# A trunk layer on one core: first two output tiles row by row, the last sums of x2 on VectorE, two PSUM banks for column tiles

## The chip, the core and the metric

The kernel runs on one core of a Trainium2 chip. The metric is the time of one execution in microseconds (us), measured on the device. A core has a matrix engine (TensorE, PE in the profile, with its weight loads as PEld), three elementwise engines (VectorE = DVE, ScalarE = ACT, GpSimd = POOL) and DMA queues, which SyncE (SP) feeds here. Matrix products land in PSUM, which has eight banks of 128 x 512 float32 values; everything else lies in SBUF.

## What is computed

One layer of a decoder trunk, for 512 positions of 2048 channels in float32:

```python
h = _rms_norm(x, norm1_g[l])
proj = h @ w_in[l]
aq, ak, av, bu, bg, cq, ck, cv = jnp.split(proj, splits, axis=-1)
...                                # A dilated attention, B GLU + conv + LayerNorm + swish, C sliding-window attention
mix = jnp.concatenate([out_a, out_b, out_c], axis=-1)
x = x + mix @ w_out[l]
h2 = _rms_norm(x, norm2_g[l])
x = x + (jax.nn.silu(h2 @ w_gate[l]) * (h2 @ w_up[l])) @ w_down[l]
```

The float32 precision is reached by splitting: every weight and operand becomes a high part (a rounded copy) and a low part (what the rounding left), and a product is a sum of several matmuls of parts.

## The kernel before

Everything lies transposed: channels on the 128 partitions, the 512 positions along the free axis. A *column tile* is 128 output channels by 512 positions and fills one PSUM bank. `mm3` (L254) adds one 128-row block of the contraction to it with three matmuls: high weight by high operand (L255), high weight by low operand (L256), low weight by high operand (L257).

Work goes in *units* of weights of 128 x 1024. A unit's weights arrive by a DMA that `pump` issues on SyncE's queue (L219); `split_up_to` makes the high part `wh` on ScalarE (L232, L237) and the low part `wl` by a subtraction on VectorE (L233, L238). From the third output tile of the second half on, that subtraction reads a second copy of the high part, `wn`, which lies in PSUM (L235, pool "high" with two buffers). `next_unit` hands a unit out and splits two units ahead.

1. **Projections** (61 units): one column tile after the other, each over 16 row blocks (`project`). Between them, as *ticks*, the mixers run. A tick is a point in the order of the program (`ticks.after(n, f)` emits f at the n-th tick from now), so a helper's place on each engine is fixed when the program is built. When a convolution pair `bu`, `bg` is there, `glu` multiplies both by the scale of the norm and with each other. The mixers' rows are the 16 row blocks c0 to a3, used in the order of `ROWS`; `split_mix` makes the high part `mh` (ScalarE) and the low part `ml` (VectorE, L746) of one.
2. **Output projection** (32 units, o tiles): half 0 uses the first eight rows for all 16 column tiles, then half 1 the other eight. `o0_n` is added to x in `residual` (L822), and `o1_n` to that (L825, tile `xr`), which gives x2. The last two mixer rows, a2 and a3, are still being computed in half 0; their matmuls, exponentials and transposes are emitted at the ticks of the first tile (one after each row) and of the others (one after each fourth row).
3. **x2's operands** during half 1: `scale_x2` makes h2 (scaled x2) and its square `sr` on ScalarE, one tick later `add_x2` makes differences of halves of h2 (`ta`, `tb`; L842 to L850), and `operands` their high and low parts (`h`, L814 on ScalarE and L815 on VectorE). These are operands of a Strassen-like scheme of seven products: `ssum2` sums the squares (L100). `add_x2` runs on GpSimd, for the very last tile (n = 15) on VectorE. `operand` q of pair j needs tiles j and j + 8, so the last pairs (6, 14) and (7, 15) come last.
4. **Gate, up and down**: for each of 44 gate and up groups and then 25 down groups, seven products in the order q = 5, 1, 7, 6, 2, 4, 3, one weight unit each, accumulate into banks `out0` to `out3` (`multiply`, L947). The weights of such a unit are sums of four blocks '11', '12', '21', '22' (GpSimd, L184; 's' is a running sum), queued in `sums` and emitted when the unit is due. For the first group, `norm2a` (after the third unit, q = 7) computes 1/rms of x2: `stat_rows` sums `ssum2` over partitions on PE (tile `n2s`, L295, in a buffer of pool "high"), VectorE scales (`n2v`, L361) and GpSimd takes the power (`n2r`, L362); `norm2b` (after the fourth unit, q = 6) spreads it over the partitions by four transposes on PE (L301).

PSUM: all eight banks are one pool (`bank`) at first, for column tiles and mixers alike, handed out in turn: a new tile waits until whatever held its bank was read. At the third o tile of half 1 the pool is closed; then four banks are `bank`'s and four hold the two buffers of "high".

Of the kernel before, what the change touches and what calls it, by code (L numbers as in the profile page):

```python
# [9 lines left out]
F32 = mybir.dt.float32  # L10
F32R = mybir.dt.float32r
# [4 lines left out]
P = 128  # L16
T = 512
# [28 lines left out]

N_SLOTS = 75

RAW_PLAIN = "22b sb 21 22a 11 sa 12".split()
# [70 lines left out]
def kernel(ctx: ExitStack, tc: tile.TileContext, xT, wi, wo, wgu, wd, cst_in, outT):  # L120
# [8 lines left out]
    def open_banks(**pools):  # L129
        if psum:  # L130
# [6 lines left out]
    open_banks(banks=8)  # L137
    ticks = Ticks()

    def slot(name, dt=F32, cols=T):  # L140
        return sp.tile([P, cols], dt, name=name, tag="s")

    def bank(name, cols=T):
        return psum["banks"].tile([P, cols], F32, name=name, tag="b")


# [5 lines left out]

    sums = defaultdict(list)
    raws, held = {}, {}

# [15 lines left out]
    def group(name, m, n, blocks):  # L171

        key = {k: (k, name) for k in ("11", "12", "21", "22", "s")}
        for k in ("21", "22", "11", "12"):
            entries.append((k + "ab"[m] if k == "22" else k, key[k], blocks[k]))
        u = len(works)

        def add(to, a, b, last=None):
            def go():
                if to == a:  # L180
                    out = raws[key[to]][0]
                else:
                    out = take("s" + "ab"[m], key[to], n)
                nc.gpsimd.tensor_add(out[:, :n], raws[key[a]][0][:, :n], raws[key[b]][0][:, :n])  # L184
                if last:
                    drop(key[last])
            return go

        sums[u - 4].append(add("s", "21", "22"))
        sums[u - 3].append(add("21", "21", "11"))  # L190
        sums[u].append(add("s", "s", "11", "11"))
        sums[u + 2].append(add("s", "s", "12"))
        works.extend((key[k], last, None) for k, last in (
            ("s", False), ("11", False), ("21", True), ("s", False), ("12", True), ("22", True), ("s", True)))
# [15 lines left out]

    splits = {}
    at = {"entry": 0, "split": 0, "use": 0}

    def pump(limit):
        while at["entry"] < len(entries) and len(raws) < limit and entries[at["entry"]][0] not in held:
            buf, key, parts = entries[at["entry"]]
            t, o = take(buf, key, sum(p.shape[-1] for p in parts)), 0
            for part in parts:
                nc.sync.dma_start(t[:, o:o + part.shape[-1]], part)  # L219
                o += part.shape[-1]  # L220
            at["entry"] += 1

    def split_up_to(i):
        while at["split"] <= min(i, len(works) - 1):
            key, last, eng = works[at["split"]]
            t, n = drop(key) if last else raws[key]
            u = at["split"]
            hi = wp.tile([P, 1024], F32R, name=f"wh{u}", tag="hi", bufs=SPLIT_BUFS)
            lo = wp.tile([P, 1024], F32R, name=f"wl{u}", tag="lo", bufs=SPLIT_BUFS)
            if eng or "high" not in psum:  # L230
                eng = eng or nc.vector
                nc.scalar.copy(hi[:, :n], t[:, :n])  # L232
                eng.tensor_sub(lo[:, :n], t[:, :n], hi[:, :n].bitcast(F32))  # L233
            else:
                near = psum["high"].tile([P, 1024], F32R, name=f"wn{u}", tag="h")  # L235
                nc.scalar.copy(near[:, :n], t[:, :n])
                nc.scalar.copy(hi[:, :n], t[:, :n])  # L237
                nc.vector.tensor_sub(lo[:, :n], t[:, :n], near[:, :n].bitcast(F32))  # L238
            splits[u] = (hi, lo)
            at["split"] += 1  # L240
# [4 lines left out]

    def next_unit():
        sums_now()
        u = at["use"]
        at["use"] += 1
        split_up_to(u + SPLIT_AHEAD)  # L250
        pump(RAW_EARLY if u < 20 else RAW_BUFS)
        return splits.pop(u)
# [111 lines left out]

    g4 = [bank(f"in{j}") for j in range(HEAD4)]
    h_hl = {}
# [30 lines left out]
    def project(name):  # L397
        b = bank(name)
        for half in range(2):
# [15 lines left out]

    def glu(j, bu, bg):
        t = slot(f"bg{j}")
        nc.vector.tensor_mul(t, bg, r1b)
        nc.scalar.activation(t, t, AF.Sigmoid)
        u = slot(f"bu{j}")  # L420
        nc.vector.tensor_mul(u, bu, r1b)
        nc.gpsimd.tensor_mul(u, u, t)
        hconv[j] = u

# [323 lines left out]

    ticks.after(1, spread_r1)
    ticks.after(2, glu, 0, g4[0], g4[1])  # L750
    ticks.after(2, glu, 1, g4[2], g4[3])
    g4 = None
# [12 lines left out]
    boxes = {"c": shared}  # L765
    part = {}
    for name in PROJ[HEAD4:]:
# [5 lines left out]
        if kind == "b":  # L773
            part[what + j] = b
            if what == "g":
                ticks.after(0, glu, int(j), part.pop("u" + j), part.pop("g" + j))
            continue
# [41 lines left out]
    def residual(n, b, half):  # L819
# [6 lines left out]
        nc.sync.dma_start(x2d[n], t)  # L826
        ticks.after(0, scale_x2, n)

    def scale_x2(n):
# [3 lines left out]
        nc.scalar.activation(sq if n else ssum2, t, AF.Square)  # L833
        ticks.after(1, add_x2, n, sq)

    def add_x2(n, sq):
        j = n % NJ
        eng = nc.gpsimd if n < KT - 1 else nc.vector
        if n < NJ:
# [4 lines left out]
        else:  # L844
# [15 lines left out]
    def split_rows(k):  # L860
        for name in ROWS[k:k + 3]:
            if name in mix:
                split_mix(name)

    load_x(0)
    load_x(1)
    late.append(True)
    for half in range(2):
        for i, n in enumerate(OUT_ORDER[half]):
            if half == 1 and i == 2:  # L870
# [30 lines left out]

    outs = [bank(f"out{i}") for i in range(4)]

# [227 lines left out]
    for g in range(2 * NP + len(DOWN)):  # L1131
# [8 lines left out]
        for i, q in enumerate(ORDER):  # L1140
# [113 lines left out]
```

## Time and profile before

| | |
|---|---|
| time, median of 3 runs (lowest, highest) | 1903.39 us (1902.68, 1906.31) |
| profiled execution: its own time, its span | 1905.27 us, 1903.5 us |
| PE busy, weight loads PEld | 1886.3 us (99%), 1638.7 us (86%) |
| DVE, ACT, POOL busy | 1443.3 us (76%), 1326.4 us (70%), 1179.6 us (62%) |
| granted PE clock, mean over the span | 0.998 of full speed |
| DMA moved | 317.67 MB, 167 GB/s |
| bytes read from HBM / written | 252.28 MB / 55.84 MB |

The first rows say how long the runs took; the profiled execution is one run more, and all durations in the text come from it. Its span covers the first to the last instruction, and the 1.8 us to its own time lie around it. The shares are averages: PE's 99% leaves about 17 us in which it had nothing to do, and the four engines are loaded differently from stage to stage. The projections end at about 411 us, the output projection at about 606 us, and the rest is the gate, up and down stage.

### The profile page before, as it was taken

How to read it: one execution, taken by the hardware profiler on the slowest of the kernel's cores; microseconds unless marked ns; L12 is line 12 of the kernel's file. 1: busy time of each engine (PE TensorE's matmuls, PEld its weight loads, DVE VectorE, ACT ScalarE, POOL GpSimd, SP SyncE). 2: the span in 40 equal slices, each digit the busy share in tenths (PEclk: the TensorE clock that was granted, in tenths of full speed). 3: DMA queues.
4: the chain of work that ended last, by engine and by line, in shares of the span. 5: the costliest groups of instructions: out<-in, count | busy, mean ns of one | idle time of the engine just before them, and what ended most of it. 6: DMA issues, size and time to landing. Idle time of an engine off the chain costs nothing.

```text
span 1903.5 us, 29681 instructions
## 1 busy us (share of the span) xinstructions
PE 1886.3 (99%) x10332; PEld 1638.7 (86%) x10332; DVE 1443.3 (76%) x2412; ACT 1326.4 (70%) x1850; POOL 1179.6 (62%) x801
## 2 busy tenths in 40 slices
PE   8999999999999999999999999999999999999999
PEld 7888888878887888888888888888888888888888
DVE  6788888997469777777777777777777866776777
ACT  6355654454356788888888888788887876767766
POOL 5134423331046787888787888788787655656777
PEclk9999999999999999999999999999999999999999
DMA  7343233323442335444454535444457766767777
GB/s 267 83 124 100 80 102 102 101 89 117 133 140 93 120 130 174 142 162 159 147 169 136 182 131 176 140 161 161 145 171 252 268 239 223 280 230 267 282 258 240
DMA packets 134246, 317.67 MB, mean 167 GB/s; under 512 B 15312, under 2 KB 30800, under 8 KB 134096
## 3 DMA queue, kind: packets, MB, share of 16 engines
q1 hardware_dynamic: 133952, 315.68, 49.5%
q8 instruction: 81, 1.33, 0.3%
q14 instruction: 69, 0.57, 0.1%
q10 hardware_dynamic: 144, 0.10, 0.0%
HBM read 252.28 MB, written 55.84 MB: 162 GB/s over the span
## 4 chain that ended last, share of the span: by engine, by line
PE 97%; DVE 2%; DMA 1%; issue 0%; SPq 0%; POOL 0%; ACT 0%; POOLq 0%; ACTq 0%; DVEq 0%
PE out L947 67%; PE o L256 3%; PE o L255 3%; PE o L257 3%; PE cq L255 2%; PE cq L257 2%; PE cq L256 2%; PE ak L255 1%; PE ak L257 1%; PE ak L256 1%; PE av L255 1%; PE av L256 1%; PE av L257 1%; PE aq L255 1%; PE aq L256 1%; PE aq L257 1%
## 5 line engine op out<-in xcount | busy, mean ns | idle before, releaser
L947 PE MATMUL out<-h,wh 128*128 128x512 f32 x2464 | 590.0, 391 | 0.9 <-DVE h L815 0.9
L947 PEld LDWEIGHTS out<-h,wh 128*128 128x128 f32 x2464 | 453.8, 189 | 89.1 <-DVE h L815 1.4
L947 PEld LDWEIGHTS out<-h,wl 128*128 128x128 f32 x2464 | 316.9, 192 | 12.0
L947 PE MATMUL out<-h,wl 128*128 128x256 f32 x2464 | 320.9, 283 | 0.0
L947 PE MATMUL out<-a,wh 128*128 128x512 f32 x1232 | 295.9, 391 | 0.0
L947 PEld LDWEIGHTS out<-a,wh 128*128 128x128 f32 x1232 | 225.8, 188 | 43.3
L232 ACT CAST wh<-w 128x1024 fp32r<-128x1024 f32 (+1 forms) x93 | 96.9, 1042 | 122.3 <-PE o L256 55.2
L947 PEld LDWEIGHTS out<-a,wl 128*128 128x128 f32 x1232 | 159.4, 191 | 6.9
L947 PE MATMUL out<-a,wl 128*128 128x256 f32 x1232 | 161.5, 283 | 0.0
L233 DVE TENSOR_TENSOR wl<-w,wh 128x1024 fp32r<-128x1024 f32 (+1 forms) x93 | 116.0, 1247 | 54.6 <-ACT wh L232 52.8
L432 DVE SCALAR_TENSOR_TENSOR y<-bu,cst,y 128x511 f32<-128x511 f32 (+14 forms) x120 | 89.9, 749 | 0.6
L960 DVE TENSOR_TENSOR y<-y,out 128x256 f32<-128x256 f32 x93 | 39.1, 420 | 43.4 <-PE out L947 37.9
L256 PE MATMUL o<-ml_c,wh 128*128 128x512 f32 x128 | 50.3, 393 | 3.1 <-DVE ml_c L746 3.1
L255 PE MATMUL cq<-hh,wh 128*128 128x512 f32 x128 | 51.2, 400 | 0.0
L255 PE MATMUL o<-mh_c,wh 128*128 128x512 f32 x128 | 51.0, 398 | 0.0
L257 PE MATMUL cq<-hh,wl 128*128 128x512 f32 x128 | 50.0, 391 | 0.0
L257 PE MATMUL o<-mh_c,wl 128*128 128x512 f32 x128 | 50.0, 391 | 0.0
L256 PE MATMUL cq<-hl,wh 128*128 128x512 f32 x128 | 49.9, 390 | 0.0
L961 DVE TENSOR_TENSOR y<-y,out 128x256 f32<-128x256 f32 x101 | 42.5, 421 | 3.5
L842 POOL TENSOR_TENSOR ta<-h 128x256 f32<-128x256 f32 x8 | 7.3, 910 | 58.5 <-issue 44.9
L354 POOL TENSOR_TENSOR ssum<-ssum,sq 128x512 f32<-128x512 f32 x15 | 25.1, 1676 | 22.4 <-ACT sq L353 22.0
L660 POOL TENSOR_SCALAR a3e<-a3e,a3d 128x128 f32<-128x128 f32 (+3 forms) x8 | 9.2, 1152 | 36.4 <-DVE a3d L658 26.8
(3125 smaller groups left out, 4998.9 us busy)
## 6 DMA issues: line engine op xcount, KB each, us to landing
a<-od SPq DMA_DIRECT2D x168, 256.0 KB, 5.4
od<-a SPq DMA_DIRECT2D x147, 256.0 KB, 4.7
w<-in_wi SPq DMA_DIRECT2D x59, 512.0 KB, 3.7
w<-in_wo SPq DMA_DIRECT2D x32, 512.0 KB, 3.6
yd<-y SPq DMA_DIRECT2D x68, 128.0 KB, 3.0
y<-yd SPq DMA_DIRECT2D x34, 256.0 KB, 5.3
x<-in_xT SPq DMA_DIRECT2D x16, 256.0 KB, 7.2
xr<-in_xT SPq DMA_DIRECT2D x16, 256.0 KB, 3.8
```

The source lines that it names most:

```text
L232: nc.scalar.copy(hi[:, :n], t[:, :n])
L233: eng.tensor_sub(lo[:, :n], t[:, :n], hi[:, :n].bitcast(F32))
L255: nc.tensor.matmul(out, wh, xh, start=start, stop=False)
L256: nc.tensor.matmul(out, wh, xl, start=False, stop=False)
L257: nc.tensor.matmul(out, wl, xh, start=False, stop=stop)
L354: eng.tensor_add(acc, acc, sq)
L432: nc.vector.scalar_tensor_tensor(yconv[j][:, i:], hconv[j][:, :T - i], c, yconv[j][:, i:], op0=ALU.mult, op1=ALU.add)
L660: nc.gpsimd.tensor_scalar(e[:, o:o + n], e[:, o:o + n], rd[:, i:i + 1], None, op0=ALU.mult)
L842: eng.tensor_sub(n1, h11, h12)
L947: nc.tensor.matmul(out, lhs[:, s], rhs, start=begin, stop=last and low == flip[0] and x is xs[-1], skip_group_check=True)
L960: sign(out, out if first is None else first, main)
L961: sign(out, out, rest)
```

## The change

1. *First two tiles row by row.* `first_two` holds o0_0 and o0_1 open together in two banks: for each of the eight rows it adds the row to both tiles, then ticks. Before, tile 0 took all eight rows with a tick after each, and tile 1 followed with two ticks.
2. *x2's last sums.* `add_x2` of pair (6, 14) moves from GpSimd to VectorE, as (7, 15) was. The `scale_x2` and `add_x2` of n = 15 come at once, without ticks between. The sums into `ssum2` of the squares of tiles 7, 14 and 15 are VectorE's. The last o tile ticks after every second row.
3. *First weight sum and copies.* The running sum 's' += '11' of the first gate group is emitted at the start of o1_15 (`first_sum`) instead of with its unit, and the `wn` copies of the next two units right after o1_15's matmuls (`near_of`).
4. *Banks.* Two banks, handed out in turn by `column`, belong to column tiles alone throughout (projections, o tiles, `out0` and `out1`, `in0`); the mixers' pool has six, and two from the third o tile of half 1 on (`out2`, `out3`).
5. `glu_u` multiplies `bu` as soon as it is there; `glu` then needs `bg` alone.
6. `norm2a` and `norm2b` run one unit later (after q = 6 and after q = 2).

```diff
+    psum["tiles"] = ctx.enter_context(tc.tile_pool(name="tiles", bufs=COLUMN_BANKS, space=bass.MemoryType.PSUM))
+    open_banks(banks=8 - COLUMN_BANKS)
...
+    def column(name):
+        return psum["tiles"].tile([P, T], F32, name=name, tag="c")
...
-        sums[u].append(add("s", "s", "11", "11"))
+        (sums[u] if name != f"g{GU_ORDER[0]}" else first_sum).append(add("s", "s", "11", "11"))
...
+    def near_of(u, t, n):
+        if u not in nears:
+            nears[u] = psum["high"].tile([P, 1024], F32R, name=f"wn{u}", tag="h")
+            nc.scalar.copy(nears[u][:, :n], t[:, :n])
...
-        ticks.after(0, scale_x2, n)
+        if n < KT - 1:
+            ticks.after(0, scale_x2, n)
+        else:
+            scale_x2(n)
...
-        eng = nc.gpsimd if n < KT - 1 else nc.vector
+        eng = nc.gpsimd if n < KT - 2 else nc.vector
...
-            ticks.after(1, operands, j, (7, n3), (6, n2), (2, h21))
+            soon = n < KT - 1
+            ticks.after(soon, operands, j, (7, n3), (6, n2), (2, h21))
             ticks.after(2, operands, j, (4, n4), (3, h22))
-        if n:
-            ticks.after(1, eng.tensor_add, ssum2, ssum2, sq)
+        if n == NJ - 1:
+            ticks.after(4, nc.vector.tensor_add, ssum2, ssum2, sq)
+        elif n:
+            ticks.after(1 if eng is nc.gpsimd else 2, eng.tensor_add, ssum2, ssum2, sq)
...
+    def first_two(*ns):
+        two = [((bank if i else column)(f"o0_{n}"), *next_unit(SPLIT_AHEAD - i)) for i, n in enumerate(ns)]
+        for k in range(8):
+            row = ROWS[k]
+            while row not in m_hi and row not in mix:
+                ticks.tick()
+            split_rows(k)
+            s = slice(k * P, (k + 1) * P)
+            for b, wh, wl in two:
+                mm3(b, wh[:, s], wl[:, s], m_hi[row], m_lo[row], k == 0, k == 7)
+            ticks.tick()
+        for i, n in enumerate(ns):
+            residual(n, two[i][0], 0)
+            load_x(i + 2)
...
-                open_banks(banks=4, high=2)
-            b = bank(f"o{half}_{n}")
+                open_banks(banks=4 - COLUMN_BANKS, high=2)
+            b = column(f"o{half}_{n}")
             wh, wl = next_unit()
+            if half == 1 and i == KT - 1:
+                first_sum.pop()()
...
-                if kk % 4 == 3 or i == 0:
+                if kk % 4 == 3 or i == 0 or (half == 1 and n == KT - 1 and kk % 2):
                     ticks.tick()
+            if half == 1 and i == KT - 1:
+                for u in range(at["split"], at["split"] + 2):
+                    near_of(u, *raws[works[u][0]])
...
-    outs = [bank(f"out{i}") for i in range(4)]
+    outs = [(column if i < COLUMN_BANKS else bank)(f"out{i}") for i in range(4)]
...
-            if g == 0 and i in (2, 3):
-                (norm2a, norm2b)[i - 2]()
+            if g == 0 and i in (3, 4):
+                (norm2a, norm2b)[i - 3]()
```

PE at the start of the output projection, before. The numbers behind names count buffers; `mh_c0` is row c0's high part, `wh61` and `wl61` are tile 0's weights, and `a2o`, `a2ph`, `a2pl` belong to the mixer row a2.

```order
L255 MATMUL o0_0_4235<-mh_c0_4146,wh61_4037 128x512
L256 MATMUL o0_0_4235<-ml_c0_4147,wh61_4037 128x512
L257 MATMUL o0_0_4235<-mh_c0_4146,wl61_4038 128x512
L700 MATMUL a2o0_4249<-a2ph00_4119,av20_3696 128x512
L701 MATMUL a2o0_4249<-a2pl00_4152,av20_3696 128x512
```

And after:

```order
L266 MATMUL o0_0_4238<-mh_c0_4149,wh61_4040 128x512
L267 MATMUL o0_0_4238<-ml_c0_4150,wh61_4040 128x512
L268 MATMUL o0_0_4238<-mh_c0_4149,wl61_4041 128x512
L266 MATMUL o0_1_4245<-mh_c0_4149,wh62_4126 128x512
L267 MATMUL o0_1_4245<-ml_c0_4150,wh62_4126 128x512
L268 MATMUL o0_1_4245<-mh_c0_4149,wl62_4127 128x512
L712 MATMUL a2o0_4256<-a2ph00_4122,av20_3699 128x512
```

Between two ticks of row a2 there now stand six matmuls of o tiles where three stood.

VectorE at the end of the output projection, before. `xr15` is x2's last tile, `o1_15` the last o tile; `wl95` is the low part of the third gate unit (q = 7), `h7_6` the operand q = 7 of pair 6.

```order
L815 TENSOR_TENSOR h5_7_5862<-ta7_5836,h5_7_5862 128x256
L825 TENSOR_TENSOR xr15_5026<-xr15_5026,o1_15_5840 128x512
L238 TENSOR_TENSOR wl95_5933<-w('21', 'g1')_5438,wn95_5934 128x1024
L815 TENSOR_TENSOR h7_6_5952<-ta6_5790,h7_6_5952 128x256
L815 TENSOR_TENSOR h6_6_5955<-tb6_5882,h6_6_5955 128x256
```

And after:

```order
L825 TENSOR_TENSOR h7_6_5883<-ta6_5793,h7_6_5883 128x256
L825 TENSOR_TENSOR h6_6_5886<-tb6_5873,h6_6_5886 128x256
L825 TENSOR_TENSOR h2_6_5889<-h2_14_5863,h2_6_5889 128x256
L101 TENSOR_TENSOR ssum2_4215<-ssum2_4215,sr7_5824 128x512
L825 TENSOR_TENSOR h4_6_5899<-tb6_5873,h4_6_5899 128x256
L825 TENSOR_TENSOR h3_6_5902<-h2_14_5863,h3_6_5902 128x256
L101 TENSOR_TENSOR ssum2_4215<-ssum2_4215,sr14_5864 128x512
L835 TENSOR_TENSOR xr15_5019<-xr15_5019,o1_15_5843 128x512
L864 TENSOR_TENSOR ta7_5839<-h2_7_5823,h2_15_5912 128x256
```

The add of the last x2 tile stood ahead of pair 6's operands and now stands behind them, behind pair 6's three differences and behind two sums into `ssum2`.

VectorE around the second norm, before. `wl97` and `wl98` are the low parts of the gate units q = 2 and q = 4, `g1u` and `g1r` sums of the group's products.

```order
L100 TENSOR_TENSOR ssum2_4212<-ssum2_4212,sr15_5963 128x512
L815 TENSOR_TENSOR h4_7_6016<-tb7_5980,h4_7_6016 128x256
L815 TENSOR_TENSOR h3_7_6019<-h2_15_5962,h3_7_6019 128x256
L955 TENSOR_REDUCE g1u_6023<-out1_5890 128x256
L238 TENSOR_TENSOR wl97_6026<-w('12', 'g1')_5642,wn97_6027 128x1024
L361 TENSOR_SCALAR n2v_6054<-n2s_6049 128x4
```

And after:

```order
L825 TENSOR_TENSOR h4_7_6010<-tb7_5916,h4_7_6010 128x256
L825 TENSOR_TENSOR h3_7_6013<-h2_15_5912,h3_7_6013 128x256
L101 TENSOR_TENSOR ssum2_4215<-ssum2_4215,sr15_5913 128x512
L998 TENSOR_REDUCE g1u_6026<-out1_5922 128x256
L249 TENSOR_TENSOR wl97_6029<-w('12', 'g1')_5645,wn97_6030 128x1024
L998 TENSOR_REDUCE g1r_6055<-out2_5923 128x256
L1003 TENSOR_TENSOR g1r_6055<-g1r_6055,out0_5921 128x256
L1004 TENSOR_TENSOR g1r_6055<-g1r_6055,out0_5921 128x256
L249 TENSOR_TENSOR wl98_6060<-w('22', 'g1')_5496,wn98_6061 128x1024
L372 TENSOR_SCALAR n2v_6086<-n2s_6081 128x4
```

The last sum of squares has moved behind h4 and h3, and `n2v`, which PE's sum of `ssum2` feeds, behind `wl98`.

More of the change, by code (lines that the diff above doesn't have):

```diff
@@ L47 @@
 N_SLOTS = 75
+COLUMN_BANKS = 2
 RAW_PLAIN = "22b sb 21 22a 11 sa 12".split()
@@ L129, in open_banks @@
     def open_banks(**pools):
-        if psum:
+        if "stack" in psum:
             psum.pop("stack").close()
@@ L135, in open_banks @@
                 tc.tile_pool(name=f"{name}{len(pools)}", bufs=bufs, space=bass.MemoryType.PSUM))
-    open_banks(banks=8)
+    psum["tiles"] = ctx.enter_context(tc.tile_pool(name="tiles", bufs=COLUMN_BANKS, space=bass.MemoryType.PSUM))
+    open_banks(banks=8 - COLUMN_BANKS)
     ticks = Ticks()
@@ L153 @@
     sums = defaultdict(list)
+    first_sum = []
     raws, held = {}, {}
@@ L209 @@
                                                   for i in range(2) for k in range(2)})
-    splits = {}
+    splits, nears = {}, {}
     at = {"entry": 0, "split": 0, "use": 0}
@@ L234, in split_up_to @@
             else:
-                near = psum["high"].tile([P, 1024], F32R, name=f"wn{u}", tag="h")
-                nc.scalar.copy(near[:, :n], t[:, :n])
+                near_of(u, t, n)
+                near = nears.pop(u)
                 nc.scalar.copy(hi[:, :n], t[:, :n])
@@ L244, in sums_now, with next_unit @@
             fn()
-    def next_unit():
+    def next_unit(ahead=SPLIT_AHEAD):
         sums_now()
@@ L249, in next_unit @@
         at["use"] += 1
-        split_up_to(u + SPLIT_AHEAD)
+        split_up_to(u + ahead)
         pump(RAW_EARLY if u < 20 else RAW_BUFS)
@@ L363, in token_scale @@
         return v, r
-    g4 = [bank(f"in{j}") for j in range(HEAD4)]
+    g4 = [(column if j < COLUMN_BANKS - 1 else bank)(f"in{j}") for j in range(HEAD4)]
     h_hl = {}
@@ L397, in project @@
     def project(name):
-        b = bank(name)
+        b = column(name)
         for half in range(2):
@@ L414, with glu_u, glu @@
     hconv, yconv = {}, {}
-    def glu(j, bu, bg):
+    def glu_u(j, bu):
+        u = hconv[j] = slot(f"bu{j}")
+        nc.vector.tensor_mul(u, bu, r1b)
+    def glu(j, bg):
         t = slot(f"bg{j}")
@@ L419, in glu @@
         nc.scalar.activation(t, t, AF.Sigmoid)
[L420 to L423, printed above, removed]
+        nc.gpsimd.tensor_mul(hconv[j], hconv[j], t)
     def tap(j, i):
@@ L749 @@
     ticks.after(1, spread_r1)
-    ticks.after(2, glu, 0, g4[0], g4[1])
-    ticks.after(2, glu, 1, g4[2], g4[3])
+    for j in range(2):
+        ticks.after(2, glu_u, j, g4[2 * j])
+        ticks.after(2, glu, j, g4[2 * j + 1])
     g4 = None
@@ L765 @@
     boxes = {"c": shared}
-    part = {}
     for name in PROJ[HEAD4:]:
@@ L773 @@
         if kind == "b":
-            part[what + j] = b
-            if what == "g":
-                ticks.after(0, glu, int(j), part.pop("u" + j), part.pop("g" + j))
+            ticks.after(0, glu if what == "g" else glu_u, int(j), b)
             continue
@@ L833, in scale_x2 @@
         nc.scalar.activation(sq if n else ssum2, t, AF.Square)
-        ticks.after(1, add_x2, n, sq)
+        if n < KT - 1:
+            ticks.after(1, add_x2, n, sq)
+        else:
+            add_x2(n, sq)
     def add_x2(n, sq):
         j = n % NJ
-        eng = nc.gpsimd if n < KT - 1 else nc.vector
+        eng = nc.gpsimd if n < KT - 2 else nc.vector
         if n < NJ:
@@ L869 @@
         for i, n in enumerate(OUT_ORDER[half]):
+            if half == 0 and i < 2:
+                if i == 0:
+                    first_two(*OUT_ORDER[0][:2])
+                continue
             if half == 1 and i == 2:
```

## The prediction

> **What bounds the kernel now.** I read the page first: the engines' shares and the chain of work that ended last.
>
> ```profile
> PE 1886.3 (99%) x10332; PEld 1638.7 (86%) x10332; DVE 1443.3 (76%) x2412; ACT 1326.4 (70%) x1850; POOL 1179.6 (62%) x801
> PE 97%; DVE 2%; DMA 1%; issue 0%; SPq 0%; POOL 0%; ACT 0%; POOLq 0%; ACTq 0%; DVEq 0%
> ```
>
> PE is busy for 1886.3 of 1903.5 us, and the change removes no matmul. So it can only act through PE's 17 us of idle time and through PE's clock. I asked next for PE's waits (engine, tile and line, what ended the wait, total us, count, mean):
>
> ```profile
> PE in L255 <- ACT wh L232: 5.3, 1, 5.3
> PE o L256 <- DVE ml_c L746: 3.1, 3, 2.5
> PE n2s L295 <- DVE ssum L100: 2.0, 1, 2.0
> PE out L947 <- DVE h L815: 0.9, 1, 0.9
> PE o L255 <- DVE xr L825: 0.9, 1, 0.9
> ```
>
> The first is the start of the program, which stays. The other four, 6.9 us, lie where the change works: the first o tile, the third tile of half 1, and the passage from the output projection to the gate stage. Then the clock, by windows of 3.41 us (window, its length, busy time of PE, PEld, DVE, ACT, POOL, then the granted clock):
>
> ```profile
> 415.68:419.10 3.42, 1.86 (x9) 1.37 (x10) 3.42 (x6) 1.14 (x3) 2.56 (x1) 1.00 0.47 95
> 545.81:551.25 5.44, 5.44 (x25) 4.51 (x24) 5.07 (x7) 3.72 (x9) 3.07 (x3) 1.00 0.41 145
> 613.66:617.07 3.41, 1.45 (x9) 1.21 (x9) 3.41 (x4) 1.54 (x2) 2.44 (x1) 1.00 0.00 0
> 617.07:623.90 6.83, 6.52 (x23) 5.90 (x24) 5.30 (x10) 1.99 (x2) 3.94 (x3) 0.50 0.26 79
> ```
>
> The clock fell to half once, for 6.83 us, behind a stretch of 3.41 us in which PE was busy for 1.45. A stretch with 1.86 busy cost nothing. So 1.96 us of idle time in 3.41 tripped it here and 1.56 did not. The fall cost half of the 6.52 busy us, 3.3. The second row is one undisturbed o tile: 24 matmuls in 5.44, 0.227 each.
>
> **First two tiles (part 1).** PE at rows c0 to c6 of tile 0 (start, duration, line, operation; in brackets the idle time before and its releaser), then VectorE:
>
> ```profile
> 411.44 0.39 PE L255 MATMUL o<-mh_c,wh 128*128 128x512 f32 x1
> 412.12 0.39 PE L700 MATMUL a2o<-a2ph,av 128*128 128x512 f32 x1
> 413.38 0.40 PE L255 MATMUL o<-mh_c,wh 128*128 128x512 f32 x1
> 416.95 0.50 PE L256 MATMUL o<-ml_c,wh 128*128 128x512 f32 x1 [2.47 <-DVE ml_c L746]
> 418.30 0.33 PE L676 MATMUL a2t<-ident,a2e 128*128 128x128 f32 x1 [0.29 <-POOL a2e L660]
> 422.23 0.50 PE L256 MATMUL o<-ml_c,wh 128*128 128x512 f32 x1 [0.21 <-DVE ml_c L746]
> 424.06 0.50 PE L256 MATMUL o<-ml_c,wh 128*128 128x512 f32 x1 [0.41 <-DVE ml_c L746]
> 416.21 1.70 DVE L746 TENSOR_TENSOR ml_c<-mix_c,mh_c 128x512 fp32r<-128x512 f32 x2
> ```
>
> Idle: 2.47+0.29+0.21+0.41 = 3.38. Row c2's low part is made on VectorE whatever PE does, and is there just before 416.95. After the change PE has six matmuls for c0, the mixer's products (412.12 to 413.38, 1.26), six for c1 and one for c2 before it needs that part: 411.44 + 13 x 0.227 + 1.26 = 415.65. It waits 1.2 to 1.3 instead of 2.47. Each later row has three more matmuls (0.68) ahead of it, more than any of the three small waits, so they go. That is 2.1 of idle time; with the slower restarts behind three gaps (the duration is 0.50 there, 0.39 elsewhere, 0.1 each) and bunched transposes I take 2.6, from 2.1 to 3.0. The a2 and a3 work comes a tile later; o tiles without a wait cover it, and without that cover the 1.2 would come back.
>
> **Banks at the third tile of half 1 (part 4).**
>
> ```profile
> 529.37 0.47 PE L255 MATMUL o<-mh_a,wh 128*128 128x512 f32 x1 [0.87 <-DVE xr L825]
> ```
>
> Here the pool of eight is closed, and the tile in the new pool waits for the add that reads the tile before. The column banks now persist, and the other bank of the two was read a tile earlier: 0.9 gained. It is lost again if the ring of two binds elsewhere (a rival below). `glu_u` (part 5) I cost at nothing: the projections show no PE wait in the list but the first, and the multiply only moves forward.
>
> **The passage into the gate stage (parts 2, 3, 4, 6).** VectorE, GpSimd and PE before:
>
> ```profile
> 600.60 1.51 DVE L815 TENSOR_TENSOR h<-ta,h 128x256 fp32r<-128x256 f32 x1
> 602.03 0.67 DVE L825 TENSOR_TENSOR xr<-xr,o 128x512 f32<-128x512 f32 x1
> 602.63 1.21 DVE L238 TENSOR_TENSOR wl<-w('11', 'g1')_5541,wn 128x1024 fp32r<-128x1024 f32 x1
> 610.74 0.41 DVE L815 TENSOR_TENSOR h<-h,h 128x256 fp32r<-128x256 f32 x1
> 611.07 0.41 DVE L848 TENSOR_TENSOR ta<-h,h 128x256 f32<-128x256 f32 x1
> 611.52 0.43 DVE L849 TENSOR_TENSOR tb<-ta,h 128x256 f32<-128x256 f32 x1
> 616.65 0.68 DVE L100 TENSOR_TENSOR ssum<-ssum,sr 128x512 f32<-128x512 f32 x1
> 600.35 1.48 POOL L100 TENSOR_TENSOR ssum<-ssum,sr 128x512 f32<-128x512 f32 x1
> 613.67 2.44 POOL L184 TENSOR_TENSOR w('s', 'g1')_5693<-w('s', 'g1')_5693,w('12', 'g1')_5642 128x1024 f32<-128x1024 f32 x1 [3.81 <-ACT h L814]
> 613.79 2.60 DVE L815 TENSOR_TENSOR h<-tb,h 128x256 fp32r<-128x256 f32 x1
> 607.51 2.00 PE L947 MATMUL out<-h,wh 128*128 128x512 f32 x8
> 610.30 2.68 PE L947 MATMUL out<-h,wh 128*128 128x512 f32 x11
> 617.38 1.87 PE L295 MATMUL n2s<-ones,ssum 128*128 128x1 f32 x8 [2.00 <-DVE ssum L100]
> 624.52 2.08 PE L947 MATMUL out<-h,wh 128*128 128x512 f32 x8
> ```
>
> An `h` subtraction takes 0.41, but 2.60 beside GpSimd's sum (613.79 beside 613.67): it ends when that ends. I carry this over. *First*, GpSimd now has the 2.4-us weight sum at 600.4, in place of the 1.48 of `ssum`; VectorE's subtraction of 600.60 ends at 603.1 instead of 602.1. Behind it stand, by the distances between starts, xr14 0.60, wl94 1.13, two h 0.68, three differences 1.25, three h 1.02, a sum 0.60, two h 0.68, a sum 0.60: 6.56. So xr15 is added from 609.7 to 610.3; before, this stood ahead of pair 6.
>
> That makes a **new wait**. The second column bank, `out1`, is o1_15's bank, so q = 1's first matmul waits for xr15's add. The eight matmuls at 607.51 are the last four of q = 5 and the first four of q = 1, so q = 1 started at 608.42; likewise q = 7 at 611.21, 2.79 a unit. Now it stalls from 608.4 to 610.3, 1.9 us; if the weight sum blocks nothing, 0.9. Three units then end at 610.3 + 8.37 = 618.7, and their operands are ready sooner (ta7 at 611.07 as before).
>
> *Second*, VectorE from 611.07: differences 1.25, wl95 1.13, three h 1.02, wl96 1.13, one h 0.34, to 615.95. The next h stands beside GpSimd's sum of '12', which waits for wl96, and ends with it at about 618.4. Then `ssum2` 0.60, a reduction 0.60, wl97 1.2: 620.85. `n2s` now stands behind `wn98` in the pool "high", so it takes the buffer of `wn97`, and PE's sum of squares waits for **wl97**, not for `ssum2` alone: 618.7 to 620.9, 2.2 us idle. What is queued behind it on PE is the whole unit q = 2. That unit ends at about 624.4; `n2v`, behind wl98, and the power give `n2r` at 624.65, the spread ends at 625.1. Before, spread and q = 2 ended at 624.52 + 2.79 = 627.3. So the stage gains 2.2 at a full clock, the cold 3.3 of before being gone; with a fall as before (idle 2.2 against the 1.96 that tripped it) it loses 0.9, the wait for `n2r` being absorbed.
>
> The Trainium skill, "TensorE: Matmul & The Clock Gate", section "Why this matters for your kernels", advises against PE-idle gaps over about 3 us, since one idle window sends the clock back to half. By that rule a gap of 2.2 does not trip it, and the sum would be the second case below. This trace speaks against the rule as a threshold: the gap of 2.00 (with 0.94 before it) tripped the clock.
>
> **Sum.** The profiled execution took 1905.27 (span 1903.5 and 1.8 around it), 1.9 above the median of 1903.39; its waits are taken as those of the median too. 2.6 + 0.9 - 0.9 = 2.6: **1900.8 us**.
>
> **The rivals.**
>
> *The clock stays up.* If the gap of 2.2 is split over two windows, or the limit is higher, the stage gains 2.2: 2.6 + 0.9 + 2.2 = 5.7, 1897.7 us. For it: 1.56 idle in a window did nothing. Against it: 1.96 did.
>
> *GpSimd goes first.* The first weight sum of the up group needs a block whose DMA is issued when wl95 has let a buffer go (613.5).
>
> ```profile
> w('22', 'u1')_5940<-in_wgu SPq DMA_DIRECT2D x1, 512.0 KB, 4.4
> ```
>
> With 0.4 of issue and 4.4 of transfer it lands at 618.3 to 618.5, just when `ssum2` wants to start at 618.4. If the weight sum starts first, `ssum2` ends with it at about 621.4 and wl97 at 623.2: idle 4.5, no gain at full clock (-0.1), and the clock surely falls (-3.1). 3.5 - 3.2 = 0.3: 1903.1 us. The Trainium skill, "SBUF — State Buffer", section "Who interferes with whom", says that issue order decides which of a two-input VectorE operation and a reading GpSimd operation blocks fully; the 2.60 above agrees. The stall of q = 1 tripping the clock as well (1.9 idle) would cost about the same.
>
> *The ring of two binds (slower).* Each o tile now waits for the add of the tile two before. VectorE's add of an `xr` needs no more than its place:
>
> ```profile
> 598.14 0.67 DVE L825 TENSOR_TENSOR xr<-xr,o 128x512 f32<-128x512 f32 x1
> 600.21 0.39 PE L255 MATMUL o<-mh_a,wh 128*128 128x512 f32 x1
> ```
>
> That add ends at 598.81, 1.4 before PE starts o1_15, the user of its bank. Once adds end over 5.44 us, one tile, after their tile, PE stalls. With VectorE 1.5 late at four tiles, 6.0, and a cold 3.3, against 3.5: 5.8 over, about 1909. Against it: pair 6's work falls on VectorE only at the last tile.
>
> *The first part does nothing*: the rows behind c2 wait as much as before because the low parts come later with the order, and the passage comes out even: 1903.4.
>
> **How the numbers follow.** Forecast 0.38; clock stays up 0.25; GpSimd first 0.19; ring 0.10; nothing 0.08. A measurement of this kernel can tell about 0.2% (3.8 us) from no change: faster is below 1899.6. The forecast's terms vary by 2 us, so a third of it is faster (0.13), all but 0.01 of the second case (0.24), together 0.37, say 0.38. Slower: the ring 0.10, and of GpSimd first with both falls and of nothing 0.06: 0.16. The rest is 0.46. The range takes in the second case with part 1 at its upper bound, 1897.7 - 0.4 - 1 for the shorter stall = 1896.3, rounded down to 1896.0, and GpSimd first with a second fall, 1903.1 + 3.1 = 1906.2, rounded to 1906.0; it leaves out the ring and the tails.
>
> **What would show it.** Right: PE's wait for ml_c falls to one of about 1.3; none for `xr` at the third tile of half 1; a new wait of `out` for `xr` near 605, of 0.9 to 1.9 us; `n2s` waiting 2 us or more for a low part `wl`. The granted clock behind it tells the forecast from the second case, the start of `ssum2`'s last sum against GpSimd's tells the third. Wrong: waits of o tiles for `xr` in half 1, or PE waits among the projections.

## The result and the profile after

The changed kernel took 1899.22 us (median of 8 runs, 1897.87 to 1901.06) against 1903.53 us (8 runs, 1902.68 to 1906.31): ratio 0.9977, 95% interval 0.9966 to 0.9988, 4.3 us less. The profiled execution took 1898.99 us; its span is 1897.2. PE's shares and waits in it, from the page and the view of waits:

```profile
PE 1883.3 (99%) x10332; PEld 1637.2 (86%) x10332; DVE 1442.8 (76%) x2417; ACT 1325.7 (70%) x1850; POOL 1173.0 (62%) x796
PE in L266 <- ACT wh L243: 5.3, 1, 5.3
PE n2s L306 <- DVE wl L249: 2.0, 1, 2.0
PE out L990 <- DVE xr L835: 1.8, 1, 1.8
PE o L267 <- DVE ml_c L758: 1.1, 1, 1.1
```

The three waits for ml_c are one of 1.1; the wait for `xr` at the third tile of half 1 is gone; two waits in the passage are new, and so is what they wait for. PE's starts of the same matmuls in the two traces show where the time went:

| point of the program | lead of the changed kernel, us |
|---|---|
| first o matmul (411.44 before, 409.90 after) | 1.54 |
| o tiles, 500 to 525 us | 4.54 |
| first gate matmul (605.65 before, 599.96 after) | 5.69 |
| rest of the gate stage, to the end | 6.28 |

So the first two tiles gave 3.0, the third tile of half 1 gave 1.15, the passage 0.6, and 1.54 stood ahead of them. Of that, 0.35 is how the program started, which differs from execution to execution (from -0.87 to 0.53 in the other traces below). The rest came at three places of the projections (208, 221 and 349 us), 0.85 of it at 349 us, where the kernel before has a wait that the changed kernel lacks:

```profile
349.48 0.33 PE L676 MATMUL a0t<-ident,a0e 128*128 128x128 f32 x1 [0.63 <-POOL a0e L660]
```

The traces show 6.3 where these medians show 4.3: the profiled execution of before was 1.7 above the median of the eight runs here. Three larger sets of runs of before, below, have medians of 1904.2 to 1904.9, so 4.3 is rather a low value. The passage after, PE's rows:

```profile
599.96 1.07 PE L990 MATMUL out<-h,wh 128*128 128x512 f32 x4
604.71 1.19 PE L990 MATMUL out<-h,wh 128*128 128x512 f32 x4 [1.80 <-DVE xr L835]
615.34 1.05 PE L306 MATMUL n2s<-ones,ssum 128*128 128x1 f32 x8 [1.98 <-DVE wl L249]
620.70 0.60 PE L312 MATMUL n2s<-ident,n2r 128*128 128x128 f32 x4
```

VectorE's and GpSimd's:

```profile
594.90 2.62 DVE L825 TENSOR_TENSOR h<-ta,h 128x256 fp32r<-128x256 f32 x1
603.98 0.68 DVE L835 TENSOR_TENSOR xr<-xr,o 128x512 f32<-128x512 f32 x1
610.32 2.63 DVE L825 TENSOR_TENSOR h<-h,h 128x256 fp32r<-128x256 f32 x1
612.88 0.68 DVE L101 TENSOR_TENSOR ssum<-ssum,sr 128x512 f32<-128x512 f32 x1
614.08 1.21 DVE L249 TENSOR_TENSOR wl<-w('12', 'g1')_5645,wn 128x1024 fp32r<-128x1024 f32 x1
594.66 2.59 POOL L190 TENSOR_TENSOR w('s', 'g1')_5696<-w('s', 'g1')_5696,w('11', 'g1')_5544 128x1024 f32<-128x1024 f32 x1
610.20 2.47 POOL L190 TENSOR_TENSOR w('s', 'g1')_5696<-w('s', 'g1')_5696,w('12', 'g1')_5645 128x1024 f32<-128x1024 f32 x1 [12.95 <-ACT h L824]
613.21 2.55 POOL L190 TENSOR_TENSOR w('s', 'u1')_6052<-w('21', 'u1')_5967,w('22', 'u1')_5969 128x1024 f32<-128x1024 f32 x1 [0.54 <-DMA w('22', 'u1')_5969<-in_wgu]
```

Each of GpSimd's first two sums holds one subtraction of VectorE until it ends. The last `xr` is added until 604.66, and q = 1 starts right behind it; wl97 ends at 615.29, and `n2s` starts right behind that. The last sum of squares starts 0.33 us ahead of GpSimd's sum for the up group. The clock, by windows:

```profile
613.82:617.23 3.41, 1.89 (x12) 1.75 (x13) 3.34 (x6) 0.00 (x0) 1.94 (x1) 1.00 0.20 38
617.23:620.64 3.41, 3.41 (x13) 2.94 (x13) 2.74 (x5) 1.99 (x2) 2.56 (x2) 0.50 0.28 115
```

It fell behind the wait at `n2s`, for 3.41 us, where it fell for 6.83 before.

### The profile page after: what moved, and what is told of

Its sections match the earlier page's. It is cut to its first block, busy times and chain, and to the rows that moved or that the text cites. A ratio compares the mean times of both kernels' runs of the same rounds, so it can differ in the third digit from the quotient of the medians.

```text
span 1897.2 us, 29702 instructions
## 1 busy us (share of the span) xinstructions
PE 1883.3 (99%) x10332; PEld 1637.2 (86%) x10332; DVE 1442.8 (76%) x2417; ACT 1325.7 (70%) x1850; POOL 1173.0 (62%) x796
## 4 chain that ended last, share of the span: by engine, by line
PE 97%; DVE 2%; issue 0%; ACT 0%; DMA 0%; POOL 0%; POOLq 0%; DVEq 0%; ACTq 0%
PE out L990 67%; PE o L267 3%; PE o L266 3%; PE o L268 3%; PE cq L266 2%; PE cq L268 2%; PE cq L267 2%; PE in L266 1%; PE in L267 1%; PE in L268 1%; PE ak L266 1%; PE ak L268 1%; PE av L268 1%; PE av L266 1%; PE av L267 1%; PE ak L267 1%
```

## The experiments

All ran beside the kernel before, in three sets of five rounds: e1, e2, e3 and e6; then e4, e5, e7 and e8; then e9 and e10. Before's median was 1904.52, 1904.21 and 1904.85 us in them, and ratios are against the before of the same set. Where a time is set against the changed kernel's 1899.22 us it stands against another set. The code fences are excerpts. The parts of the change come first, on the kernel before.

**e1, the first two tiles alone.**

```diff
+            if half == 0 and i < 2:
+                if i == 0:
+                    first_two(*OUT_ORDER[0][:2])      # both tiles from bank()
+                continue
```

> The kernel before with part 1 alone (two tiles row by row, both in the old pool of eight banks). Theory: PE's waits for ml_c fall from 3.1 us in three to one of about 1.1 us, as in the whole change, and the time falls by 3.0 us (2.4 to 3.3) against the kernel before, to about 1900.5; the passage into the gate stage keeps its waits of 0.9 for h and 2.0 for ssum and its fall of the clock. Rival (the order makes the low parts come later): the waits for ml_c stay near 3 us and the time moves by less than 1 us.

1901.41 against 1904.52 us, ratio 0.9985 (0.9976 to 0.9994): 3.1 us. PE's waits:

```profile
PE n2s L295 <- DVE ssum L100: 2.0, 1, 2.0
PE o L256 <- DVE ml_c L746: 1.1, 1, 1.1
PE out L966 <- DVE h L815: 0.9, 1, 0.9
PE o L255 <- DVE xr L825: 0.9, 1, 0.9
PE a0t L676 <- POOL a0e L660: 0.6, 1, 0.6
```

Behind the start of the program only the waits for ml_c changed, and the 0.3 of `a2t` beside them is gone. The gain of the first part is its own (2.97 us of the trace's lead arise there), and it is not given back.

**e2, the column banks (and `glu_u`) alone.**

```diff
+    open_banks(banks=8 - COLUMN_BANKS)                # and psum["tiles"] with two
...
-        b = bank(name)
+        b = column(name)
...
-    outs = [bank(f"out{i}") for i in range(4)]
+    outs = [(column if i < COLUMN_BANKS else bank)(f"out{i}") for i in range(4)]
```

> The kernel before with parts 4 and 5 alone (two column banks, six and later two for the rest, bu multiplied at once). Theory: the wait of 0.9 us for xr at the third tile of half 1 goes (1.2 us of time with its restart), and so does the 0.6 us that a0t waited for a0e in the projections if that came from the shared pool; the last add of xr still stands ahead of pair 6's operands and ends about 2 us before q = 1 starts, so the second column bank costs nothing here. Time 1.2 to 2.0 us below before. Rival (the ring of two binds): waits of o tiles or of out for xr of over 0.5 us in sum, and no gain.

1902.42 against 1904.52 us, ratio 0.9989 (0.9981 to 0.9998): 2.1 us. Its waits behind the start of the program:

```profile
PE o L261 <- DVE ml_c L752: 2.5, 1, 2.5
PE n2s L300 <- DVE ssum L101: 2.0, 1, 2.0
PE out L951 <- DVE h L819: 0.9, 1, 0.9
PE a2t L682 <- POOL a2e L666: 0.3, 1, 0.3
```

Neither `a0t` nor `xr` is waited for. In its trace 0.85 us came at 349 us and 1.15 at 529 us. The ring of two never bound an o tile. The 2.1 us are in spite of a second fall of the clock in this trace: behind the wait of 2.5 for ml_c it was at half from 416.51 to 419.92, where before's stayed up.

What made `a0t` wait is GpSimd's operation for it, beside VectorE's tap of the convolution (`y`). Before, then after:

```profile
346.20 0.74 DVE L432 SCALAR_TENSOR_TENSOR y<-bu,cst,y 128x507 f32<-128x507 f32 x1
346.24 3.19 POOL L660 TENSOR_SCALAR a0e<-a0e,a0d 128x512 f32<-128x512 f32 x1 [2.35 <-ACT mix_a L709]
```

```profile
345.24 1.77 POOL L672 TENSOR_SCALAR a0e<-a0e,a0d 128x512 f32<-128x512 f32 x1 [2.06 <-PE aq1f L494]
345.49 1.17 DVE L444 SCALAR_TENSOR_TENSOR y<-bu,cst,y 128x507 f32<-128x507 f32 x1
```

Where VectorE's operation starts first, GpSimd's takes 3.19 us (3.18 and 3.17 in e1 and e3); where GpSimd's starts first, it takes 1.77 (also in e2) and VectorE's is the longer one. Parts 4 and 5 together turn the order round. Which of the two does it, and why, no run shows.

**e3, the sums, copies and the later norm alone**, in the old banks.

```diff
-        eng = nc.gpsimd if n < KT - 1 else nc.vector
+        eng = nc.gpsimd if n < KT - 2 else nc.vector
...
-            if g == 0 and i in (2, 3):
+            if g == 0 and i in (3, 4):
```

These are two of its edits; it has all of parts 2, 3 and 6.

> The kernel before with parts 2, 3 and 6 alone (x2's last sums on VectorE, first weight sum and copies sooner, second norm a unit later), in the old banks, where q = 1's bank is not the last o tile's. Theory A (VectorE's chain from the last xr to wl97 is what PE waits for): the stall of q = 1 for xr is absent, but PE then waits about as long for the operands of pair 7 and for wl97, 3.5 to 4.0 us in sum, and the time is within 1 us of before. Theory B (the stall for the bank was a cost of its own): the sum of the waits is about 2.0 us and the time 2.0 to 2.5 us below before.

1905.04 against 1904.52 us, ratio 1.0003 (0.9994 to 1.0012). PE's waits in the passage:

```profile
PE n2s L301 <- DVE wl L244: 2.2, 1, 2.2
PE out L967 <- ACT wh L243: 1.2, 1, 1.2
```

Without the bank's wait PE waits 1.2 us for `wh95`, which ScalarE makes behind its work on the last x2 tile, and 2.2 for wl97: 3.4 in sum. Theory A holds for the time and nearly for the sum, though it named the operands of pair 7 and not ScalarE's copy: these parts by themselves give nothing that can be measured. Here too the clock fell behind the wait for ml_c, at 417.68, besides the fall behind `n2s`.

**e6, other banks for out1 and out3** in the changed kernel.

```diff
-    outs = [(column if i < COLUMN_BANKS else bank)(f"out{i}") for i in range(4)]
+    outs = [(column if i in (0, 3) else bank)(f"out{i}") for i in range(4)]
```

> The changed kernel with out1 in the mixers' pool and out3 in the column pool, so that q = 1's bank is not the last o tile's. Theory A (VectorE's chain is what PE waits for): the 1.8 us for xr goes, and waits for the operands of pair 7 and for wl97 grow by as much; time within 0.7 us of the changed kernel's (about 1899.2). Theory B (the bank's wait was a cost of its own): 1.5 to 1.8 us below the changed kernel's, about 1897.5, with the wait for wl97 still 2.0.

1899.43 us (9 runs), ratio 0.9974 (0.9965 to 0.9984), the changed kernel's time: its 1.8 for `xr` became the same 1.2 and 2.2 as in e3. The profiled execution was the slowest of the nine, 1901.70. The bank's wait was no cost of its own; VectorE's chain, with ScalarE's behind it, sets the time.

**e4 and e9, where n2s's buffer comes from.** In e4 the tile is asked for ahead of the split that takes wn98, in e9 it is also written there.

```diff
+    def norm2_buffer():
+        n2["b"] = psum["high"].tile([P, 1024], F32, name="n2s", tag="h")
+        nc.scalar.copy(n2["b"][:, T:T + 4], nhalf[:, :4])      # e9 only
...
+            if g == 0 and i == 3:
+                norm2_buffer()
             w = next_unit()
```

> The changed kernel with n2s's buffer taken from the pool before the next near copy (wn98) instead of after it, so that the sum of squares waits for ssum2 and wn98 for wl97. Theory (the wait is for the buffer): PE's wait at n2s falls from 2.0 us to 0.2 to 0.3, no window of half clock follows it, and a wait of 1 to 1.5 us for n2r or for unit q = 4's weights takes part of its place; time 0.5 to 2.5 us below the changed kernel's. Rival (ssum2 is what it waits for): the wait at n2s stays 2.0 and the time as the changed kernel's, about 1899.2.

> The changed kernel with n2s taken from the pool ahead of wn98 and at once written in four spare columns by ScalarE, so that the buffer is really handed out there: n2s now takes wn96's buffer and wn98 that of wn97 (asking for it earlier without writing left every instruction's wait as it was). Theory (the wait is for the buffer): the sum of squares waits for ssum2 alone, PE's wait falls from 2.0 to 0.2 to 0.5 us; wn98 and so n2v and n2r come about 1.5 us later, and PE waits 1 to 1.6 us for n2r instead; time 0.3 to 2 us below the changed kernel's (1898.1 to 1899.2). Rival (ssum2 itself is late): the wait at n2s stays above 1.5 us.

e4 came out with the changed kernel's instructions, buffer for buffer and in the same order on every engine: asking sooner, without writing, moved nothing. So it is a second measurement of that kernel, 1898.09 us (5 runs), ratio 0.9967 (0.9955 to 0.9980). Its median is 1.1 us below the first, and 6.1 below before in its own set where the first was 4.3 below: two such medians can lie that far apart. The forecasts of e4, of a shorter wait by another buffer, are not tested by it. e9 took 1898.35 us, ratio 0.9967 (0.9955 to 0.9979). PE in e4, then in e9:

```profile
605.28 1.94 PE L992 MATMUL out<-h,wh 128*128 128x512 f32 x4 [1.81 <-DVE xr L835]
615.90 1.05 PE L306 MATMUL n2s<-ones,ssum 128*128 128x1 f32 x8 [0.45 <-DVE wl L249]
```

```profile
604.81 1.19 PE L993 MATMUL out<-h,wh 128*128 128x512 f32 x4 [1.80 <-DVE xr L835]
614.85 0.95 PE L306 MATMUL n2s<-ones,ssum 128*128 128x1 f32 x8
619.25 0.65 PE L312 MATMUL n2s<-ident,n2r 128*128 128x128 f32 x4 [0.54 <-POOL n2r L373]
```

In both the clock fell earlier, right behind the stall of q = 1, so PE came to `n2s` about 1.5 us later. In e4 `n2s` still starts at the end of wl97, so its wait is shorter only because PE comes later. In e9 it waits for nothing and starts at 614.85, while wl97 runs until 615.37; `n2r` is late by 0.54. The buffer was the wait, but at this place in the queue it is worth no more than two medians differ.

**e5, the weight sum of '12' behind the last sum of squares**, by one column that GpSimd reads from it first.

```diff
+                if behind:
+                    nc.gpsimd.tensor_sub(early, behind()[:, :1], behind()[:, 1:2])
-        sums[u + 2].append(add("s", "s", "12"))
+        sums[u + 2].append(add("s", "s", "12", behind=(lambda: ssum2) if name == f"g{GU_ORDER[0]}" else None))
```

> The changed kernel with a one-column GpSimd operation that reads the finished ssum2 put ahead of GpSimd's weight sum of '12', so that this sum starts behind VectorE's last subtraction and last sum of squares. Theory (VectorE's chain to wl97 is held up for 2.2 us by that weight sum, and PE by the chain): the 2.63 us subtraction takes 0.4, the wait at n2s falls from 2.0 to under 0.3, no half clock follows, and n2r comes 0.8 us late because GpSimd's sums stand ahead of it; time 2 to 3.5 us below the changed kernel's, about 1896.5. Rival (the chain has other holds): the wait at n2s stays over 1.5 us and the time within 0.5 us of 1899.2.

1897.01 us (5 runs), ratio 0.9960 (0.9948 to 0.9973): 2.2 below the changed kernel's median, 1.1 below e4's in the same set, whose lowest run (1897.76) is above the highest here (1897.51). VectorE, GpSimd and PE:

```profile
610.35 0.42 DVE L827 TENSOR_TENSOR h<-h,h 128x256 fp32r<-128x256 f32 x1
611.59 2.40 POOL L192 TENSOR_TENSOR w('s', 'g1')_5696<-w('s', 'g1')_5696,w('12', 'g1')_5645 128x1024 f32<-128x1024 f32 x1
613.22 0.98 PE L308 MATMUL n2s<-ones,ssum 128*128 128x1 f32 x8
617.39 0.65 PE L314 MATMUL n2s<-ident,n2r 128*128 128x128 f32 x4 [0.30 <-POOL n2r L375]
```

The subtraction of 2.63 takes 0.42, the wait at `n2s` is gone, and the clock does not fall in this trace. The stall of q = 1 is still 1.81, and in three of the five runs the mean granted clock is 0.999, as in the changed kernel with its one fall.

**e7, the sums of '11' and '12' in quarters.**

```diff
+                parts = 4 if name == f"g{GU_ORDER[0]}" and to == a == "s" else 1
+                for c in range(parts):
+                    s = slice(c * n // parts, (c + 1) * n // parts)
+                    nc.gpsimd.tensor_add(out[:, s], raws[key[a]][0][:, s], raws[key[b]][0][:, s])
```

> The changed kernel with GpSimd's two additions into the first gate group's running sum ('11' and '12') cut into four pieces of 256 columns each. Theory (a VectorE subtraction is held until the one GpSimd instruction beside it ends): both 2.6 us subtractions fall to at most 1.2 us, the last xr is added 1.5 us sooner, the stall of q = 1 falls from 1.8 to about 0.3 us and the wait at n2s to about 1; time 2.5 to 4.5 us below the changed kernel's. Rival (the two engines share the rate, whatever the pieces): the subtractions or those behind them take as long in sum, both waits stay within 0.4 us, time as 1899.2.

1895.35 us (5 runs), ratio 0.9953 (0.9941 to 0.9966): 3.9 below the changed kernel, 2.7 below e4. The two subtractions, a sum of squares beside the second sum, GpSimd's sum of '11', and PE:

```profile
594.85 0.95 DVE L828 TENSOR_TENSOR h<-ta,h 128x256 fp32r<-128x256 f32 x1
608.82 0.96 DVE L828 TENSOR_TENSOR h<-h,h 128x256 fp32r<-128x256 f32 x1
609.71 1.23 DVE L101 TENSOR_TENSOR ssum<-ssum,sr 128x512 f32<-128x512 f32 x1
594.59 3.22 POOL L193 TENSOR_TENSOR w('s', 'g1')_5696<-w('s', 'g1')_5696,w('11', 'g1')_5544 128x256 f32<-128x256 f32 x4
603.22 1.21 PE L993 MATMUL out<-h,wh 128*128 128x512 f32 x4 [0.37 <-DVE xr L838]
612.72 1.05 PE L309 MATMUL n2s<-ones,ssum 128*128 128x1 f32 x8 [0.83 <-DVE wl L252]
```

VectorE is held for one piece, not for the whole sum; GpSimd pays 0.6 us more for it (3.22 against 2.59). Both stalls shrink, and the mean granted clock is 1.000 in all five runs. The traces of e5 and e7 have one wait more, of 0.9 and 0.8 for a weight's low part, far behind at 1788 us; e8 and e10 lack it, and its cause was not sought.

**e8, '11' in quarters and '12' behind ssum2**, with the edit of e5 besides this one.

```diff
+                parts = 4 if name == f"g{GU_ORDER[0]}" and to == a == "s" and last else 1
```

> The changed kernel with the addition of '11' in quarters (as above) and that of '12' whole but behind ssum2 (as above). Theory: the two gains add as far as PE can use them; the stall of q = 1 about 0.3 us, no wait at n2s, one of about 1 us for n2r; time 3.5 to 5.5 us below the changed kernel's, about 1895, and below both kernels. Rival (something else is late next, a weight copy or n2r): PE waits 2 us or more there and the time is no lower than that with '12' behind ssum2 alone.

1894.73 us (5 runs), ratio 0.9950 (0.9936 to 0.9963). `n2s` waits for nothing, the stall of q = 1 is 0.4, `n2r` is 0.3 late. It is 3.4 below e4; against e7 it is 0.6, less than two medians can differ by.

**e10, as e8, and unit 63's split behind row c2.**

```diff
-        two = [((bank if i else column)(f"o0_{n}"), *next_unit(SPLIT_AHEAD - i)) for i, n in enumerate(ns)]
+        two = [((bank if i else column)(f"o0_{n}"), *next_unit(1 - i)) for i, n in enumerate(ns)]
...
+            if k == 2:
+                split_up_to(at["use"])
```

> The kernel with '11' in quarters and '12' behind ssum2, and besides the split of unit 63 (the third o tile's weights) moved in the two first tiles from their start to behind row c2, so that VectorE makes c2's low part ahead of wl63 (1.2 us). Theory (the 1.1 us that is left of the wait for ml_c is VectorE's place in the queue, not the row itself): the wait falls to 0.4 us or less and the time by 0.5 to 1.1 us, to about 1894. Rival (c2's row itself is late, or wl63 is late next): a wait of over 0.8 us for ml_c or for a weight stays, and the time is as without.

1894.04 us (5 runs, 1893.60 to 1894.35), ratio 0.9944 (0.9931 to 0.9956): the fastest of all, 10.8 us below before in its set and 5.2 below the changed kernel's median. PE's waits:

```profile
PE in L271 <- ACT wh L248: 6.2, 1, 6.2
PE out L997 <- DVE xr L840: 0.3, 1, 0.3
PE n2s L317 <- POOL n2r L378: 0.3, 1, 0.3
PE a2t L693 <- POOL a2e L677: 0.2, 1, 0.2
```

The 1.1 for ml_c was VectorE's place in its queue (wl63 stood ahead), not the row: the wait is gone, and in the trace the first two tiles give 3.8 us against e8's 3.0. The medians of e8 and e10 are from two sets and differ by only 0.7. Behind the start of the program PE now waits less than 1 us in all by this list.

## Why the prediction was right

The forecast was 1900.8 us in a range of 1896.0 to 1906.0; it came to 1899.22, 1.6 us lower. The range takes in the time before too, so the time by itself tests little; the waits below test more.

- *First two tiles*: one wait of 1.2 to 1.3 was forecast, 1.12 is there; 2.6 us, where the trace has 3.0 and e1 3.1. The bunched transposes and restarts were worth their upper bound.
- *Third tile of half 1*: 0.9 forecast, 1.15 in the trace: the 0.87 of waiting and a restart.
- *The new wait of q = 1*: 1.9 forecast, 1.80. The mechanism, GpSimd's earlier sum beside the subtraction and the last `xr` behind pair 6, is the one in the rows above.
- *The wait of n2s for wl97*: 2.2 forecast, 1.98.
- *GpSimd goes first* was the third case. The last sum of squares started 0.33 us ahead of GpSimd's sum for the up group; a dead heat had been forecast, and that it fell on the forecast's side was luck.
- *The ring of two* bound no o tile, in any run.

Two terms were mis-sized. **The clock's fall** was priced at 6.83 us of half clock, so that the passage lost 0.9; it lasted 3.41, and the passage gained 0.6. The runs show that the price is a matter of where the gap falls. The same stall of 1.80 at q = 1 brought the clock down in e4 and e9 (at 605.5 and 606.3) but not in e5 and not in the changed kernel; the equal waits of 2.15 at `n2s` cost 3.41 us of half clock in e3 and 6.83 in e6. The mean granted clock of the single runs tells the same, a window of 3.41 at half being 0.0009 of it: of 31 runs of before 24 had 0.998 (median 1904.4), five 0.997 (1905.1) and two 0.996 (1905.3); of the changed kernel's eight, seven had 0.999 and one 1.000, its fastest, 1897.87. But this mean does not order the runs by itself: in e4 and e9 those with 1.000 (1898.08; 1897.95 and 1899.35) were no faster than the others. So the forecast's case and the case in which the clock stays up look less like two cases than like one with a spread. The rule of the Trainium skill, "TensorE: Matmul & The Clock Gate", section "Why this matters for your kernels", would have let a gap of 2 us pass; the fall behind 1.98 us in the trace after, and behind 1.80 in e9, speaks against it.

**The projections** were costed at nothing, on the word that PE has no wait there but the first. The list of waits has one, 0.6 for `a0t`, below the rows that were quoted. With the column banks and `glu_u` alone it goes (e2), and 0.85 us with it. In the traces the gain is 6.3 us against the 2.6 forecast, and these two terms (1.5 and 0.85) are the larger part of the difference. The medians give 4.3 and, in e4, 6.1. All the misses lie on one side: each term came out better than forecast.

That the passage gains little was in the forecast, which had it at a loss of 0.9; e3 bears this out for parts 2, 3 and 6 by themselves. They move work from GpSimd to VectorE, which is nearly full there (busy for 3.34 of 3.41 us at 613.82), and start a GpSimd sum at a time when VectorE's operation beside it must wait. The gain of the change is that of its part 1 and of its parts 4 and 5, which were not run apart.

## What to carry to other kernels

Ask of each operation that is moved to an idle engine, or earlier, which operation of the busy engine will run beside it: here one GpSimd instruction of 2.5 us held a 0.4-us subtraction until it ended, and cutting it into four, or starting it behind the busy engine's chain, gained more than moving it had: 2.7 and 1.1 us against the same kernel in the same set (e4), where the move gave nothing that could be measured (e3). A wait that names a bank or a buffer may only be the first of a chain to be noticed; take it away alone, as in e6, and see whether the time follows before counting it. And read the list of waits to its end, at the places where nothing is expected too.

## What the runs showed of the hardware

In each kept trace the clock changes only at points a whole number of 3.41 us apart, on a grid that the program does not set: it lies elsewhere in each execution. Gaps of 1.8 us of PE's time are enough for a fall if they lie badly on it. The changed kernel and e4 run the same instructions with the same stall at q = 1, from 602.91 to 604.71 and from 603.47 to 605.28. Here are the window of the grid in which the stall ends and the window behind it, first in the changed kernel, then in e4:

```profile
603.57:606.98 3.41, 2.27 (x14) 2.05 (x15) 2.55 (x6) 2.70 (x5) 0.00 (x0) 1.00 0.21 77
606.98:610.40 3.42, 3.42 (x21) 2.97 (x20) 3.42 (x7) 3.42 (x8) 0.20 (x1) 1.00 0.35 69
```

```profile
602.05:605.46 3.41, 1.60 (x10) 1.08 (x9) 3.17 (x8) 2.70 (x6) 0.00 (x0) 1.00 0.00 0
605.46:608.87 3.41, 3.41 (x13) 3.03 (x14) 2.79 (x6) 3.41 (x7) 0.00 (x0) 0.50 0.21 77
```

In the changed kernel the border at 603.57 parts the stall in two and the clock stays up; in e4 one window holds all of it and the clock falls. The same holds for the wait of 2.5 for ml_c: before, the border at 415.68 parts it (2.20 and 1.86 us busy, no fall); in e2 and e3 one window holds it (1.06 and 0.94 busy) and the clock falls. So the first part of the change takes away a place at which the clock can fall, too.

In the twelve traces, after the clock's first rise, every window of the grid that had the full clock and PE busy for 1.61 us or less was followed by half clock, and none with 2.1 or more was. In between lie two: 1.89 brought the clock down in the changed kernel, and 1.86 did not at 415.68 in the kernel before. The former held eight matmuls of one column, the latter only wider ones, of 128 columns and more; whether narrow matmuls count less was not tried. The length of a fall goes the same way. Four falls lasted 6.83 us, behind `n2s` in before, e1, e2 and e6: there the eight narrow matmuls stand in the first window of half clock (PE busy for 2.91 to 3.27 us). Six lasted 3.41 us (the changed kernel, e2's and e3's first, e3's second, e4, e9): none of them holds these matmuls in its window, with PE busy for 3.21 to 3.41. The five runs each of the kernels without such gaps (e7, e8, e10) spread over 0.8 to 1.0 us, the eight of before over 3.6.

The other finding is that a block between VectorE and GpSimd has the length of one instruction: 2.62 us beside a whole sum, 0.95 beside one in quarters, 0.42 with none. The Trainium skill, "SBUF — State Buffer", section "Who interferes with whom", has the block and its rule of issue order, which the rows bear out, those of `a0e` under e2 for both orders.
